# A second product of the down projection made of halved blocks, on one Trainium2 core

## The chip, the cores and the metric

The kernel runs on one core of a Trainium2 chip. The time is device microseconds (us) of one execution. Five engines run beside each other, each through its own list of instructions in order: TensorE (PE; its weight loads are listed apart as PEld), VectorE (DVE), ScalarE (ACT), GpSimd (POOL) and SyncE (SP), which here only issues transfers. Between them stand semaphores. Most transfers between DRAM and the on-chip memory are issued by SP, one behind the other.

## The reference

A decoder block in float32: sequence 1024, model width 1024. A pooling mixer and a sliding-window attention are merged by gates, then comes an MLP. The change touches only the MLP's two ends:

```python
    h2 = _rmsnorm(x, g_mlp_pre[l])
    ff = jnp.einsum('bsf,fd->bsd',
                    jnp.square(jax.nn.relu(jnp.einsum('bsd,df->bsf', h2, w_up[l]))), w_down[l])
    x = x + _rmsnorm(ff, g_mlp_post[l])
```

with w_up 1024 x 4096 and w_down 4096 x 1024. f below is the squared ReLU, 1024 x 4096.

## The kernel before

**Float32 out of faster passes.** Each operand of a matmul is split into a high and a low part of a reduced 32-bit format: `split` (L99) makes the high part by a CAST on ACT (L101) and the low part by a subtraction on DVE (L104). A product is then three passes: high by high, f's high by the weights' low, f's low by the weights' high (`PASSES`).

**Seven products instead of eight.** "Up" (the product with w_up) and "Down" (with w_down) are each made of 2 x 2 blocks, by a scheme that needs 7 products of half-size blocks and sums of blocks ahead of and behind them. Up's close, `up_close0` (L1614), forms the seven left operands out of f and stores them, 512 wide, into a scratch tensor in DRAM, `f_dram`; Down reads them back. The right operands are blocks B11, B12, B21, B22 of w_down or sums of them, made on DVE in the place where the blocks lie.

**Down.** Product i runs through 8 steps of the contraction, 56 steps in all, `PRODUCTS = (1, 5, 2, 3, 6, 7, 4)` (L2158). A usual step is 24 matmuls of 512 columns: 2 slices k2, 4 output tiles t, 3 passes (`down_mm`, L2071, matmuls recorded at L2075). The two parts of the left operand lie in tiles `wh`, those of the right in `ar`: six tiles of each, so three pairs. At step j, `ahead(j)` calls `operands` (L1963) for step j+2: SP loads the left block into a `raw` tile (four of them), ACT and DVE split both operands. A pair's tiles come free when the step that uses them ends.

**The sixth product** is not made so: its 512 x 512 blocks are halved once more and the same scheme is used within it, seven products of 256-wide blocks, `quarters` (L2021) for the operands, `quarters_mm` (L2043, matmuls at L2055) and `quarters_close` (L2059). A step is then 42 matmuls of 256 columns. Its operands are four sets of splits a step: f1 (128 x 1024, from `raw`), f2 (128 x 768, sums of quarters that Up has stored, from `raw`), w1 (128 x 512 and 128 x 256, from B11) and w2 (128 x 1024, from T, the sums of B11's quarters). They take two pairs of `wh` and two of `ar`, out of the same three.

**What sets the order.** A scheduler orders each engine's instructions from the program's order and its own costs, but where `manual_schedule` stands, DVE's follow the program's text: in Down before, for the operands of products 6, 7 and 4. `differences` (L2003), the sums of the blocks of w_down for products 3 to 4, is called all at once at the seventh step of product 3, and the scheduler spreads it over products 2 and 3. Product 3 adds onto product 5's banks of the accumulator memory, product 2 onto product 1's.

**Behind the products** come sums of their results, the norm's squares and gains (`fin_half`, `after_sixth`, `after_seventh`, `fin_out`), and for the last tile `last_tile` (L2124), whose DVE instructions end the execution.

## Time and profile before

| | us |
|---|---|
| median of 3 runs (1090.56 to 1091.35) | 1091.15 |
| the profiled execution's own time | 1091.0 |
| its span, first to last instruction | 1089.2 |
| PE busy | 1079.7 (99%) |
| DVE busy | 849.2 (78%) |
| ACT busy | 625.5 (57%) |
| Down, first matmul to PE's last | 779.1 to 1081.6 |
| the sixth product | 953.2 to 993.7 |

The page's first part sums each engine's busy time, the second shows it in 40 slices, the fourth follows the end back through what released it. A row of a timeline is: start, duration, engine, line, operation, output<-inputs, shape, how many in a row, and in square brackets the idle time ahead of it and what ended it. Pieces that follow each other on an engine overlap by some 0.1 us, as the pipeline does, so a cost in a row of work is read from start to start.

### The profile page before, as it was taken

The page shows a single profiled execution, that of the slowest core. Times are in us where ns is not written, and L with a number is a line of the kernel's source. Part 1 is how long each engine was busy: PE and PEld are TensorE (multiplying, and loading weights), DVE is VectorE, ACT ScalarE, POOL GpSimd, SP SyncE. Part 2 cuts the span into 40 slices and gives each one's busy share as a digit, 9 for nine tenths or more (in the row PEclk, how much of TensorE's full clock was granted, in tenths as well). Part 3 has the DMA queues.
Part 4 walks back from the last instruction along what each step waited for, and adds up shares of the span by engine and source line. Part 5 has one row for each costly group of instructions (what it writes and reads, how often), then busy time and mean ns, then how long its engine had stood idle before and what let it go on. Part 6 is the DMA issues. An engine that isn't in the chain of part 4 may idle for free.

```text
span 1089.2 us, 14332 instructions
## 1 busy us (share of the span) xinstructions
PE 1079.7 (99%) x5211; PEld 903.5 (83%) x5211; DVE 849.2 (78%) x1194; ACT 625.5 (57%) x1029; POOL 86.2 (8%) x142
## 2 busy tenths in 40 slices
PE   9999999999999999999999999999999999999997
PEld 8888888888888888888888888888888888898885
DVE  6688888989897887889876766665657867579996
ACT  7567886456654257567665554555446535476543
POOL 0354411100100012100000000000000000000000
PEclk9999999999999999999999999999999999999999
DMA  9666889679965776832566534445597873379622
GB/s 333 201 174 175 214 251 350 184 233 315 268 213 171 223 191 137 288 117 77 185 227 227 205 143 174 160 150 216 177 391 272 299 265 118 101 234 318 218 78 78
DMA packets 100921, 227.36 MB, mean 209 GB/s; under 512 B 10481, under 2 KB 28017, under 8 KB 100849
## 3 DMA queue, kind: packets, MB, share of 16 engines
q1 hardware_dynamic: 84416, 189.46, 50.8%
q0 software_dynamic: 10528, 16.78, 8.8%
q10 hardware_dynamic: 5904, 20.19, 4.8%
q8 instruction: 41, 0.67, 0.3%
q14 instruction: 32, 0.25, 0.1%
HBM read 161.38 MB, written 63.97 MB: 207 GB/s over the span
## 4 chain that ended last, share of the span: by engine, by line
PE 75%; DVE 4%; ACT 1%; issue 1%; DMA 1%; ACTq 0%; DVEq 0%
PE mm L583 18%; PE at L583 15%; PE at L2075 12%; PE mm L2075 11%; PE mm L1523 5%; PE mm L494 3%; PE at L2055 2%; PE at L1523 2%; PE at L1251 2%; PE mm L2055 2%; PE mm L1251 1%; PE mm L496 1%; PE at L1569 1%; DMA st<-in_w_g_dram 1%; DVE xf L2121 0%
## 5 line engine op out<-in xcount | busy, mean ns | idle before, releaser
L2075 PE MATMUL at<-ar,wh 128*128 128x512 f32 x552 | 126.0, 389 | 0.2 <-DVE ar L104 0.2
L2075 PEld LDWEIGHTS at<-ar,wh 128*128 128x128 f32 x552 | 103.4, 188 | 22.1 <-DVE ar L104 0.6
L2075 PE MATMUL mm<-ar,wh 128*128 128x512 f32 x528 | 120.5, 389 | 0.0
L2075 PEld LDWEIGHTS mm<-ar,wh 128*128 128x128 f32 x528 | 99.1, 188 | 20.5
L101 ACT CAST wh<-raw 128x1024 fp32r<-128x1024 f32 (+1 forms) x58 | 59.2, 1023 | 86.2 <-PE at L2075 37.0
L104 DVE TENSOR_TENSOR wh<-st,wh 128x512 fp32r<-128x512 f32 (+1 forms) x103 | 74.4, 733 | 38.9 <-ACT wh L101 34.3
L104 DVE TENSOR_TENSOR wh<-raw,wh 128x1024 fp32r<-128x1024 f32 (+1 forms) x58 | 68.4, 1186 | 40.8 <-ACT wh L101 40.6
L583 PE MATMUL mm<-T,wx 128*128 128x512 f32 x375 | 90.3, 389 | 0.0
L583 PEld LDWEIGHTS mm<-T,wx 128*128 128x128 f32 x375 | 70.4, 188 | 14.6
L583 PE MATMUL mm<-gr,wh 128*128 128x512 f32 x321 | 77.2, 391 | 0.0
L101 ACT CAST wh<-st 128x512 fp32r<-128x512 f32 (+2 forms) x102 | 65.8, 654 | 19.2 <-PE at L583 4.6
L583 PEld LDWEIGHTS mm<-gr,wh 128*128 128x128 f32 x321 | 59.9, 188 | 12.2
L583 PE MATMUL mm<-T,wh 128*128 128x512 f32 x267 | 66.0, 389 | 0.0
L104 DVE TENSOR_TENSOR ar<-B,ar 128x1024 fp32r<-128x1024 f32 (+2 forms) x51 | 50.9, 1011 | 14.7 <-ACT ar L101 14.4
L583 PE MATMUL at<-gr,wh 128*128 128x512 f32 x243 | 59.0, 389 | 0.0
L583 PE MATMUL mm<-x,wh 128*128 128x512 f32 x240 | 58.9, 394 | 0.0
L583 PEld LDWEIGHTS mm<-T,wh 128*128 128x128 f32 x267 | 50.1, 188 | 10.4
L101 ACT CAST ar<-B 128x1024 fp32r<-128x1024 f32 (+2 forms) x51 | 44.1, 882 | 19.3 <-PE mm L2055 6.4
L583 PEld LDWEIGHTS at<-gr,wh 128*128 128x128 f32 x243 | 45.6, 188 | 9.5
L583 PEld LDWEIGHTS mm<-x,wh 128*128 128x128 f32 x240 | 44.2, 188 | 9.6 <-ACT f L692 0.2
L583 PE MATMUL at<-T,wx 128*128 128x512 f32 x213 | 52.0, 389 | 0.0
L583 PEld LDWEIGHTS at<-T,wx 128*128 128x128 f32 x213 | 40.0, 188 | 8.3
(529 smaller groups left out, 2264.5 us busy)
## 6 DMA issues: line engine op xcount, KB each, us to landing
raw<-f_dram SPq DMA_DIRECT2D x52, 512.0 KB, 4.7
B<-in_w_dn_dram SPq DMA_DIRECT2D x32, 512.0 KB, 6.5
f_dram<-g SPq DMA_DIRECT2D x28, 512.0 KB, 2.8
st<-in_w_up_dram SPq DMA_DIRECT2D x24, 512.0 KB, 4.5
g<-spill_dram SPq DMA_DIRECT2D x17, 512.0 KB, 5.7
f_dram<-g ACTq DMA_DIRECT2D x17, 512.0 KB, 2.9
st<-in_w_g_dram SPq DMA_DIRECT2D x16, 512.0 KB, 4.7
g<-in_w_up_dram SPq DMA_DIRECT2D x15, 512.0 KB, 4.8
```

The source lines that it names most:

```text
L101: act.copy(hi, src)
L104: return eng.tensor_tensor(lo, src, f32(hi), ALU.subtract)
L494: pe.matmul(bs[th], whi[:, k, :], rhs(k, hl, th), start=k == 0 and hl == 0, stop=False)
L496: pe.matmul(bs[th], wlo[:, k, :], rhs(k, 0, th), start=False, stop=k == nk - 1)
L583: pe.matmul(b, w[wh][:, kt, :], x_, start=not after and kt == 0 and j == 0, stop=kt == 3 and j == 2, skip_group_check=after)
L1251: pe.matmul(b, w[wh][:, kt, :], xo[xh][:, kt, :], start=not after and kt == 0 and j == 0, stop=kt == 1 and j == 2, skip_group_check=after)
L1523: pe.matmul(bs[t], Am[a][k][ah][:, t * P:(t + 1) * P], Wm[w][k][wh], start=not after and k == 0 and j == 0, stop=k == 3 and j == 2, skip_g ...
L1569: pe.transpose(b[:, i, :], hs[4 * th + i][:, k * P:(k + 1) * P], ident)
L2055: pe.matmul(part[q][:, t, :], o[fs][fh][:, fk, t * P:(t + 1) * P], o[ws][wh][:, wk, :], start=q not in ONTO and (s_, t, j) == (0, 0, 0), s ...
L2075: pe.matmul(bs[t], fo[fh][:, k2, t * P:(t + 1) * P], wo_[wh][:, k2, :], start=not after and s2 == 0 and k2 == 0 and j == 0, stop=(s2, k2) ...
```

## The change

It does six things.

- The products' order is 1, 2, 5, 3, 6, 7, 4, and the fifth too is made as seven products of halved blocks (steps 16 to 23; the sixth stays at 32 to 39). `quarters`, `quarters_mm` and `quarters_close` take the product's number. The fifth's close writes four tiles `v4`.
- Up stores quarters' sums for the fifth as well as for the sixth (`e_dram(i, s)`), and splits the left operands of products 7 and 3 into high and low itself, in place; `f_dram` grows from 7 to 9 blocks. In Down the operands of these two products are loaded straight into `wh`, 2 x 512 KB a step (`WITH_PARTS`), where before one 512-KB load into `raw` was followed by a split.
- DVE's order in the whole of Down follows the text. The sums of blocks are called step by step: `first_sum` (B11 from B12 and B11) at steps 8 to 15, `quarter_sums` (T, three instructions) at 9 to 16 and 26 to 33, `next_sum` (B12, then B11) at 16 to 19 and 22 to 29, `last_sum` at 42 to 49.
- Loads of the weights' blocks are issued by a table of steps (`LOADS`), behind the load of that step's left operand.
- The tiles lie elsewhere: `raw` moves to the pool `rp`, B21, B22 and T share eight tiles "x".
- Product 3 has accumulator banks of its own and is added to v4 on DVE; the gains of `fin_half` and the squares of x1 move to steps 33 to 36 and 24 to 31; the operands of product 4's last three steps are made in another order.

```diff
             if m // 2 % 2 == 0:
-                dve.tensor_tensor(s2[:, 256:], s2[:, :256], s2[:, 256:], ALU.subtract)
-                s2_even.append(s2)
+                for b in (t[:, 0, :], s2):
+                    dve.tensor_tensor(b[:, 256:], b[:, :256], b[:, 256:], ALU.subtract)
+                evens.append(t)
             else:
-                a = s2_even.pop()
-                e = g32([3, 256])
-                dve.tensor_tensor(e[:, 1, :], s2[:, 256:], a[:, 256:], ALU.subtract)
-                dve.tensor_tensor(e[:, 0, :], e[:, 1, :], a[:, :256], ALU.add)
-                dve.tensor_tensor(e[:, 2, :], s2[:, :256], e[:, 1, :], ALU.subtract)
-                q.dma_start(e_dram(m // 4), e)
-            q.dma_start(fd[:, 4:6, :], t)
-            q.dma_start(fd[:, 0:2, :], f.rearrange("p (a b) -> p a b", b=512))
-            q.dma_start(fd[:, 6, :], s4)
+                t0 = evens.pop()
+                for i, a, b in ((5, t0[:, 0, :], t[:, 0, :]), (6, t0[:, 1, :], s2)):
+                    e = g32([3, 256])
+                    dve.tensor_tensor(e[:, 1, :], b[:, 256:], a[:, 256:], ALU.subtract)
+                    dve.tensor_tensor(e[:, 0, :], e[:, 1, :], a[:, :256], ALU.add)
+                    dve.tensor_tensor(e[:, 2, :], b[:, :256], e[:, 1, :], ALU.subtract)
+                    q.dma_start(e_dram(i, m // 4), e)
+            q.dma_start(fd[:, 5:7, :], t)
+            q.dma_start(fd[:, 0, :], f[:, :512])
+            for c, hi, lo in ((1, g[:, :512], f[:, 512:]), (7, s4[:, :512], s4[:, 512:])):
+                split(hi.bitcast(F32R), lo.bitcast(F32R), lo)
+                if c == 1:
+                    q.dma_start(fd[:, 1, :], hi)
+                    q.dma_start(fd[:, 2, :], lo)
+                else:
+                    q.dma_start(fd[:, 7:9, :], s4.rearrange("p (a b) -> p a b", b=512))
...
-    A_OF = {1: 0, 7: 1, 2: 2, 4: 3, 5: 4, 6: 5, 3: 6}
+    A_OF = {1: 0, 7: 1, 2: 3, 4: 4, 5: 5, 6: 6, 3: 7}
+    WITH_PARTS = (7, 3)
...
-    rpool = tc.tile_pool(name="rp", bufs=24, side="right", reuse_waits="tile")
+    rpool = tc.tile_pool(name="rp", bufs=16, side="right", reuse_waits="tile")
...
-        return dl.tile([P] + shape, F32, tag="raw", name=nm("raw"), bufs=4)
+        return rp.tile([P] + shape, F32, tag="raw", name=nm("raw"), bufs=4)
...
+    def held(name, dt=F32):
+        return dl.tile([P, 2, 512], dt, tag="x", name=nm(name), bufs=8)
...
+        if i in WITH_PARTS:
+            fo = wslot([2, 512]), wslot([2, 512])
+            for c, t in enumerate(fo):
+                behind[:] = [nc.sync.dma_start(f32(t), f_block(A_OF[i] + c, s_))]
+            ft = None
+        elif i == 1 and s_ in early_raw:
...
-    def differences(s_):
-        b11, b12, b22 = (res[n, s_] for n in ("B11", "B12", "B22"))
-        dve.tensor_tensor(b11, b22, b11, ALU.subtract)
-        w = halved(b11)
-        dve.tensor_tensor(b12, b22, b12, ALU.subtract)
-        tt = res["T", s_] = rp.tile([P, 4, 256], F32, tag="w", name=nm("T"))
+    def first_sum(s_):
+        dve.tensor_tensor(res["B11", s_], res["B12", s_], res["B11", s_], ALU.subtract)
+
+    def next_sum(n, s_):
+        dve.tensor_tensor(res[n, s_], res["B22", s_], res[n, s_], ALU.subtract)
+
+    def last_sum(s_):
+        dve.tensor_tensor(res["B11", s_], res["B21", s_], res["B11", s_], ALU.subtract)
+
+    def quarter_sums(s_):
+        w = halved(res["B11", s_])
+        tt = res["T", s_] = dl.tile([P, 4, 256], F32, tag="x", name=nm("T"), bufs=8)
         dve.tensor_tensor(tt[:, 0:2, :], w[:, 1::2, :], w[:, 0:2, :], ALU.subtract)
...
-        order = (5, 6, 1, 7, 3, 2, 4) if s_ == 0 else (5, 6, 3, 1, 7, 2, 4)
+    def quarters_mm(i, s_):
+        o = opers[i, s_]
+        onto = ONTO if i == 6 else {}
+        order = (5, 6, 3, 1, 7, 2, 4)
         if s_ == 0:
-            for q in (5, 6, 1, 7, 3, 2, 4):
-                part[q] = bank("mm" if q in ONTO else "at", [2, 256])
-                if q in ONTO:
+            order = (5, 6, 1, 7, 3, 2, 4) if i == 5 else (5, 6, 1, 3, 7, 2, 4)
+            mine, other = ("mm", "at") if i == 5 else ("at", "mm")
+            for q in order:
+                part[q] = bank(other if q in ONTO else mine, [2, 256])
+                if q in onto:
                     act.copy(part[q], block_of(u4, *ONTO[q]))
...
+        t4 = u4 if i == 6 else v4
+        w = block_of(t4, 2, 1)
         act.copy(a, part[1])
         dve.tensor_tensor(c, a, part[6], ALU.add)
         dve.tensor_tensor(e, c, part[5], ALU.add)
-        w = block_of(u4, 2, 1)
-        dve.tensor_tensor(w, w, part[5], ALU.add)
-        dve.tensor_tensor(d, c, part[7], ALU.add)
+        if i == 6:
+            dve.tensor_tensor(w, w, part[5], ALU.add)
+            dve.tensor_tensor(d, c, part[7], ALU.add)
+        else:
+            dve.tensor_tensor(d, c, part[7], ALU.add)
+            dve.tensor_tensor(w, d, part[5], ALU.add)
         for q, s in ((3, e), (2, a), (4, d)):
-            dve.tensor_tensor(block_of(u4, *ONTO[q]), s, part[q], ALU.add)
-        behind[:] = [dve.tensor_tensor(w, w, d, ALU.add)]
...
-    PRODUCTS = (1, 5, 2, 3, 6, 7, 4)
+    PRODUCTS = (1, 2, 5, 3, 6, 7, 4)
+    HALVED = (5, 6)
...
-        if (i, s_) == (3, NS - AHEAD):
-            for s2 in range(NS):
-                differences(s2)
...
+    TAGS = {1: ("at",) * 4, 3: ("at", "mm", "mm", "mm"), 7: ("mm", "at", "at", "at"), 4: ("at", "mm", "mm", "mm")}
+    banks = {}
+
+    LOADS = (("B11", 4, 3), ("B12", 5, 8), ("B22", 14, 8), ("B21", 41, 8))
+
+    def loads(j):
+        for name, first, n in LOADS:
+            if 0 <= j - first < n:
+                later(name, j - first)
+
+    def sums(j):
+        def at(first):
+            return 0 <= j - first < NS
+        if at(8):
+            first_sum(j - 8)
+        if at(9):
+            quarter_sums(j - 9)
+        if 16 <= j < 20 or 24 <= j < 28:
+            next_sum("B12", j - 16 - j // 24 * 4)
+        if at(22):
+            next_sum("B11", j - 22)
+        if at(26):
+            quarter_sums(j - 26)
+        if at(42):
+            last_sum(j - 42)
+
+    def ends(j):
+        if 33 <= j < 37:
+            fin_half(j - 33, 0, c11[j - 33])
+        if 24 <= j < 24 + NS:
+            square_x1(j - 24)
+        if j == 36:
+            scaled_eps()
+        if 40 <= j < 44:
+            after_sixth(j - 40)
+        if j in OUT_AT:
+            fin_out(OUT_AT.index(j), (c11, c12))
+        if 48 <= j < 52:
+            after_seventh(j - 48, banks[7][j - 48])
+
+    OUT_AT = (44, 45, 46, 47)
...
+    def ahead(j):
+        if j == 50:
+            operands(*steps[52])
+            operands(*steps[54])
+            operands(*steps[55])
+        elif j == 51:
+            operands(*steps[53])
+        elif j < 50:
+            operands(*steps[j + AHEAD])
...
+    with tc.manual_schedule(engines={mybir.EngineType.DVE}):
+        for j in range(1, AHEAD):
+            operands(*steps[j])
+        for j, step in enumerate(steps[:-1]):
+            down_step(j, *step)
+    down_step(len(steps) - 1, *steps[-1])
```

**The places in the order.** DVE in the sixth product before; B are blocks of w_down, T the quarters' sums, wh and ar the splits' outputs. Each step is f2, w2, w1 (two), f1:

```order
L104 TENSOR_TENSOR wh_8258<-raw_8243,wh_8257 128x1024
L104 TENSOR_TENSOR wh_8297<-raw_8294,wh_8296 128x768
L104 TENSOR_TENSOR ar_8299<-T_8201,ar_8298 128x1024
L104 TENSOR_TENSOR ar_8305<-B_1092_7125,ar_8304 128x512
L104 TENSOR_TENSOR ar_8305<-B_1092_7125,ar_8304 128x256
L104 TENSOR_TENSOR wh_8307<-raw_8292,wh_8306 128x1024
L104 TENSOR_TENSOR wh_8350<-raw_8347,wh_8349 128x768
L104 TENSOR_TENSOR ar_8352<-T_8207,ar_8351 128x1024
L104 TENSOR_TENSOR ar_8358<-B_1099_7163,ar_8357 128x512
L104 TENSOR_TENSOR ar_8358<-B_1099_7163,ar_8357 128x256
L104 TENSOR_TENSOR wh_8360<-raw_8345,wh_8359 128x1024
```

Splits alone stand here, step behind step. In the change, DVE in the fifth product, from f1 of step 17 on (L2020 to L2022 are `quarter_sums`, L2012 is `next_sum`):

```order
L104 TENSOR_TENSOR wh_7819<-raw_7804,wh_7818 128x1024
L2020 TENSOR_TENSOR T_7856<-B_1113_7374 128x512
L2021 TENSOR_TENSOR T_7856<-B_1113_7374,T_7856 128x256
L2022 TENSOR_TENSOR T_7856<-B_1113_7374,T_7856 128x256
L2012 TENSOR_TENSOR B_1119_7386<-B_1192_7773,B_1119_7386 128x1024
L104 TENSOR_TENSOR wh_7866<-raw_7863,wh_7865 128x768
L104 TENSOR_TENSOR ar_7868<-T_7620,ar_7867 128x1024
L104 TENSOR_TENSOR ar_7874<-B_1126_7424,ar_7873 128x512
L104 TENSOR_TENSOR ar_7874<-B_1126_7424,ar_7873 128x256
L104 TENSOR_TENSOR wh_7876<-raw_7861,wh_7875 128x1024
L2012 TENSOR_TENSOR B_1127_7426<-B_1204_7826,B_1127_7426 128x1024
L104 TENSOR_TENSOR wh_7940<-raw_7937,wh_7939 128x768
```

Between f1 of step 17 and f2 of step 18 stand four sums of blocks, and one L2012 more stands ahead of f2 of step 19; two further ones stand alike ahead of f2 of steps 20 and 21. In the change's sixth product, from f1 of step 33 to f2 and w2 of step 34:

```order
L104 TENSOR_TENSOR wh_8718<-raw_8703,wh_8717 128x1024
L2020 TENSOR_TENSOR T_8725<-B_1100_7300 128x512
L2021 TENSOR_TENSOR T_8725<-B_1100_7300,T_8725 128x256
L2022 TENSOR_TENSOR T_8725<-B_1100_7300,T_8725 128x256
L2020 TENSOR_TENSOR T_8732<-B_1106_7336 128x512
L2021 TENSOR_TENSOR T_8732<-B_1106_7336,T_8732 128x256
L2022 TENSOR_TENSOR T_8732<-B_1106_7336,T_8732 128x256
L104 TENSOR_TENSOR wh_8741<-raw_8738,wh_8740 128x768
```

Two steps' quarter sums stand here between the splits, where before none did; one more such group of three stands ahead of step 35's f2, one L2099 (a gain of `fin_half`) ahead of each of the f2 of steps 36 to 39, and four small instructions (`scaled_eps`) ahead of the last of these.

SP where the seventh product's first loads stand before (L1969; B are B21's blocks):

```order
L1969 DMA raw_8757<-f_dram 128x2x512
L1953 DMA B_1394_8932<-in_w_dn_dram 128x2x512
L1969 DMA raw_8868<-f_dram 128x2x512
L1969 DMA raw_8881<-f_dram 128x2x512
L1953 DMA B_1395_8934<-in_w_dn_dram 128x2x512
```

and SP where the third product's first loads stand in the change, behind the fifth's last ones:

```order
L2030 DMA raw_8203<-spill_dram 128x768
L1965 DMA B_1267_8157<-in_w_dn_dram 128x2x512
L1965 DMA B_1278_8223<-in_w_dn_dram 128x2x512
L1979 DMA wh_8268<-f_dram 128x2x512
L1979 DMA wh_8269<-f_dram 128x2x512
L1979 DMA wh_8373<-f_dram 128x2x512
L1979 DMA wh_8374<-f_dram 128x2x512
```

Two loads a step, L1979, go into `wh`, where before one into `raw` stood; so too for the seventh.

More of the change, by code (lines that the diff above doesn't have):

```diff
@@ L2102, in square_x1 @@
         t = flat(raw_tile())
-        nc.sync.dma_start(t, x1_dram[n])
+        with tc.issue_after(behind[0].ins):
+            nc.sync.dma_start(t, x1_dram[n])
         act.activation(t, t, AF.Square, scale=ROOT_D, accum_out=nsq[:, n:n + 1])
@@ new lines, in down_step @@
+    def down_step(j, i, s_):
+        last = s_ == NS - 1
+        normal = [(s_, k2, t) for k2 in range(2) for t in range(4)]
+        if i in HALVED and last:
+            with tc.manual_schedule(engines=CORE):
+                quarters_mm(i, s_)
+                quarters_close(i)
+            ahead(j)
+            sums(j)
+        elif i == 3 and last:
+            down_mm(i, s_, banks[i], False, normal)
+            for t in range(4):
+                dve.tensor_tensor(c12[t], v[t], banks[i][t], ALU.add)
+            ahead(j)
+            sums(j)
+        else:
+            sums(j)
+            ahead(j)
+        loads(j)
+        if i in HALVED:
+            if not last:
+                quarters_mm(i, s_)
+            ends(j)
+            return
+        if s_ == 0 and i in TAGS:
+            banks[i] = [bank(tag) for tag in TAGS[i]]
+        bs = banks[1 if i == 2 else i]
+        if (i, s_) != (3, NS - 1) and (i != 4 or s_ < NS - LATE):
+            down_mm(i, s_, bs, i == 2, normal[:3] + normal[4:7] if (i, s_) == (4, NS - LATE - 1) else normal)
+        ends(j)
+        if not last:
+            return
```

151 lines of the change are left out of this document (40 added, 111 removed).

## The prediction

> **What bounds the kernel now.** I read the page's first two parts, the stages' windows, the chain of waits over Down, then the engines' timelines there.
>
> ```profile
> PE 1079.7 (99%) x5211; PEld 903.5 (83%) x5211; DVE 849.2 (78%) x1194; ACT 625.5 (57%) x1029; POOL 86.2 (8%) x142
> PE   9999999999999999999999999999999999999997
> 953.00:994.00 41.00, 41.00 (x340) 40.81 (x339) 32.62 (x39) 32.14 (x45) 0.00 (x0) 1.00 0.78 255
> 994.00:1038.00 44.00, 43.79 (x193) 35.82 (x192) 42.72 (x56) 23.20 (x31) 0.00 (x0) 1.00 0.73 252
> ```
>
> PE works without a gap nearly to the end, so the time is the sum of its matmuls. Two things can count: cheaper or fewer matmuls, and gaps on PE that were not there. In the windows' rows (length, then busy PE, PEld, DVE, ACT, POOL, granted clock, DMA's share, GB/s) DVE is next behind PE in Down: busy 32.6 of 41 us in the sixth product, 42.7 of 44 after it. The chain of waits over Down shows each product's price:
>
> ```profile
> 779.30 43.52 PE at L2075 x192
> ...
> 909.86 43.52 PE mm L2075 x192
> 953.38 2.87 PE at L2055 x24
> ...
> 993.85 4.30 PE at L2075 x19
> 998.15 1.14 DVE wh L104
> 999.28 1.15 DVE ar L104
> 1000.47 37.47 PE at L2075 x164
> 1037.94 32.22 PE mm L2075 x142
> ```
>
> A usual product is 192 matmuls in 43.52 us, so 0.2267 us each and 5.44 us a step. The halved sixth lasts from 953.38 to 993.85, 40.47 us for 336 matmuls, so 0.120 us each and 5.04 us a step. The seventh, from 993.85 to 1037.94, takes 44.09 us: 0.57 more than 43.52, and two splits on DVE are in the chain there. They are the operands of its second step, behind the eight instructions of the sixth's close.
>
> **What a halved step leaves free on DVE.** This decides the forecast. DVE in the sixth, and ACT's row for the same kind of operand:
>
> ```profile
> 968.51 1.03 DVE L104 TENSOR_TENSOR ar<-B,ar 128x512 fp32r<-128x512 f32 x2
> 969.45 2.10 DVE L104 TENSOR_TENSOR wh<-raw,wh 128x1024 fp32r<-128x1024 f32 x2
> 971.47 1.22 DVE L104 TENSOR_TENSOR ar<-T,ar 128x1024 fp32r<-128x1024 f32 x1
> 973.54 1.03 DVE L104 TENSOR_TENSOR ar<-B,ar 128x512 fp32r<-128x512 f32 x2 [0.86 <-ACT ar L101]
> 962.81 0.93 ACT L101 CAST ar<-B 128x512 fp32r<-128x512 f32 x2 [1.26 <-PE mm L2055]
> ```
>
> From one w1 to the next, 968.51 to 973.54, are 5.03 us, a step. Of these 0.86 are idle, so the four sets of splits take 4.17. The idle time cannot be moved: w1 of the next step takes the tiles of this step's w1, ACT waits for PE to be done with them late in the step (1.26 in its row), and DVE for ACT. The operands begin at the step's end and must be done one step later. So a halved step has 0.86 us for other work on DVE; what exceeds it delays the next step's operands, and PE, which has nothing else to do, by as much. (A piece costs DVE some 0.09 less than its duration: the 1.03 at 968.51 is followed at 969.45.)
>
> **The change part by part.**
>
> 1. The fifth product halved: 43.52 becomes 336 x 0.120 = 40.3, so -3.2 us. The price of a halved matmul is seen in this trace:
>
> ```profile
> 953.22 3.04 PE L2055 MATMUL at<-ar,wh 128*128 128x256 f32 x24
> 956.09 2.32 PE L2055 MATMUL mm<-ar,wh 128*128 128x256 f32 x18
> ```
>
> 24 matmuls take 2.87 us from start to start, 0.120 each. The Trainium skill, "TensorE: Matmul & The Clock Gate", "Back-to-back issue gap", gives 262 cycles for 256 columns, an estimate of 0.109 us for each, but says too that in a stream the weight loads set the spacing as well. By 0.109 the fifth would take 36.7 and the saving be 6.9; the trace has 0.120 in the very stream that the change adds a second time, so the trace decides and the page's figure gets no chance of its own.
>
> 2. Sums of blocks between the halved splits. What they cost, from the groups of Down:
>
> ```profile
> L2007 DVE TENSOR_TENSOR B<-B,B 128x1024 f32<-128x1024 f32 x8 | 9.8, 1220 | 0.0
> L2009 DVE TENSOR_TENSOR T<-B 128x512 f32<-128x512 f32 x8 | 5.5, 690 | 0.2
> L2011 DVE TENSOR_TENSOR T<-B,T 128x256 f32<-128x256 f32 x8 | 3.4, 424 | 0.2
> L2010 DVE TENSOR_TENSOR T<-B,T 128x256 f32<-128x256 f32 x8 | 3.4, 422 | 0.2
> L2084 DVE TENSOR_TENSOR c<-c,bc 128x512 f32<-128x512 f32 x8 | 5.5, 690 | 1.6 <-ACT junk L2081 1.5
> 1079.83 0.16 DVE L144 TENSOR_TENSOR frr<-sm,sm 128x1 f32<-128x1 f32 x1
> ```
>
> Less 0.09 each: a block's sum 1.13, three quarter sums 0.60 + 0.33 + 0.33 = 1.27 (rounded), a gain 0.60; the small ones 0.16. In the changed order the fifth has T and a sum ahead of step 18's f2, 2.40, which is 1.54 over the 0.86, and one sum ahead of each of steps 19, 20 and 21, 0.27 over, 0.81 together: +2.35. The sixth has two T ahead of step 34's f2, 2.54, 1.68 over; one T ahead of step 35's, 0.41 over; a gain ahead of 36 to 38's, 0.60, which fits; a gain and four small ones ahead of 39's, 0.60 + 0.64, 0.38 over: +2.45. Together +4.8. A stall shifts every later step, DVE's splits too, so each counts in full. From below it is 0, if the splits can run further ahead than I read (rival A); from above 10.8, if none of the 0.86 can be used (2.40 + 3 x 1.13 + 2.54 + 1.27 + 1.24). The rows show the 0.86 idle in step after step and free for any work that needs no new operand, so I take 4.8. The sums also wait for their blocks of w_down, with all splits behind them on DVE; these are asked for two steps ahead, 10 us, and a block lands 5.5 us after its issue (quoted under 4): no wait. ACT's copies and squares of product 2's results, now between the first splits of the fifth, could make step 17 late by less than one copy, 0.59; taken as 0, since PE then waits a step earlier and DVE catches up by as much at step 18.
>
> 3. From the sixth to the seventh. Left operands come by DMA and only one split, 1.13, waits behind the close, where before two pairs stood in the chain; the 0.57 above should go: -0.6.
>
> 4. Loads straight into wh. At the third's and the seventh's first step the tiles come free only when step 22 or 38 ends, and 1 MB must land within one halved step, 5.04 us. The nearest rows are two loads issued 0.41 apart (start on SP's queue, and to landing):
>
> ```profile
> 869.47 0.37 SPq L1969 DMA_DIRECT2D raw<-f_dram  x1
> 869.88 0.46 SPq L1953 DMA_DIRECT2D B<-in_w_dn_dram  x1
> raw<-f_dram SPq DMA_DIRECT2D x1, 512.0 KB, 4.6
> B<-in_w_dn_dram SPq DMA_DIRECT2D x1, 512.0 KB, 5.5
> ```
>
> The high part, 4.6, is there in time. The low one lands 0.41 + 5.5 = 5.9 after the first issue; the step's third matmul wants it at 5.04 + 0.45. So 0.4 late each time with the traffic of those rows, nothing with an idle queue: from 0 to 0.9 each (0.9 if the weights' loads stand ahead), 0.15 taken, since the loads ahead of them in SP's list are a step older: +0.3. The Trainium skill, "DMA: Bandwidth & Descriptors", "Measured", has 6.15 us for 1 MB, another path; by it the loads would come 0.7 late each, +1.4. Later steps have two steps' time. Behind such a load SP has only x1's loads and the next step's, which have that time too.
>
> 5. The tail.
>
> ```profile
> 1077.39 0.68 DVE L2262 TENSOR_TENSOR u<-u,mm 128x512 f32<-128x512 f32 x1
> 1081.36 0.68 DVE L2139 TENSOR_TENSOR u<-u,mm 128x512 f32<-128x512 f32 x1
> 1080.68 0.88 PE L2136 MATMUL at<-hold,hold 128*128 128x256 f32 x6
> ```
>
> DVE's chain for the third of the last tiles takes 3.97 us, and last_tile's first sum follows it 0.2 ahead of PE's end. In the changed order the three tiles' chains stand wholly one behind the other, where before the first two were interleaved, and 15 instead of 18 matmuls of 512 columns lie behind the third tile's last: 0.68 us less cover. From 0 to 0.7, 0.45 taken.
>
> 6. Up's additions, in each of the 14 pairs (f's squares at L1663): two splits of 512, and one or three sums of 256. Prices, count and cover:
>
> ```profile
> L104 DVE TENSOR_TENSOR wx<-ws,wx 128x512 fp32r<-128x512 f32 x30 | 20.4, 687 | 0.0
> L101 ACT CAST wx<-ws 128x512 fp32r<-128x512 f32 x30 | 17.9, 618 | 7.7 <-DVE ws L535 6.1 <-PE at L583 1.6
> L1663 ACT ACTIVATE g<-g 128x1024 f32<-128x1024 f32 x14 | 14.9, 1061 | 0.1
> 600.00:700.00 100.00, 100.00 (x443) 82.84 (x442) 65.54 (x107) 53.74 (x86) 0.00 (x0) 1.00 0.48 174
> 700.00:779.00 79.00, 79.00 (x350) 65.42 (x349) 46.83 (x72) 40.82 (x61) 0.00 (x0) 1.00 0.49 178
> ```
>
> That is 2 x 0.60 + up to 3 x 0.33 = 2.2 us on DVE and 1.24 on ACT, some ten and six us more in 100, where DVE is idle for 34 and ACT for 46; the instructions stand behind the pair's close, whose results only Down reads, and what queues behind them, the next pair's splits, is made a pair ahead. Taken 0; rival C is the price without that cover. In the second and third products a step of 5.44 us holds three pieces of 1.13 and a T of 1.27, 4.66: it fits. The tiles' new places move no work on PE.
>
> Sum against the profiled execution's 1091.0, 0.15 under the median shown: 1091.0 - 3.2 + 4.8 - 0.6 + 0.3 + 0.45 = 1092.75, so **1092.7 us**.
>
> **The rivals.** A, the sums cost nothing: DVE's idle time lies wherever it is needed, since ACT may run further ahead than the rows show. 1092.75 - 4.8 = 1088.0. For it: DVE is busy for only 32.6 of 41 in the sixth, and 4.8 of other work would fill 37.4. Against it: the same idle 0.8 in every step, always ahead of w1 and for PE's sake; it cannot be saved up.
>
> B, slower: the loads into wh. They can only be issued when PE leaves the tiles, one step ahead. If both transitions get 5.9 or more, and the transfers are slowed by what is left of the blocks' loads, 0.9 each: 1092.75 - 0.3 + 1.8 = 1094.25. The point is a landing 5.5 us behind the issue of the first. For it: the row with 5.9. Against it: 512 KB alone lands within 4.6, and SP's queue has little ahead of them.
>
> C, Up: the added work makes a split late for PE in each of the 14 pairs by half of one, 0.3: 1092.75 + 4.2 = 1096.95. Against it: in Up's two rows PE is busy in every microsecond, with DVE idle for a third.
>
> **How the numbers follow.** The forecast has 0.50, A 0.22, B 0.21, C 0.07. The forecast alone spans 1091 to 1094: a third of the 4.8 either way, the tail's and the loads' ends within that. The range that leaves out no more than 2 in 10 goes from A, 1088.0, to past B, 1095.0; what lies outside are A's lower half, C, and the sums' upper bound. A measurement here cannot tell less than 0.2% from no change, 2.2 us: 1088.97 to 1093.33. Faster: A but for 0.02. Slower: B, C and 0.06 of the forecast's upper edge, 0.34. Same: the other 0.44 of the forecast and A's 0.02, 0.46.
>
> **What would show it.** Right: the fifth's matmuls at 0.120, 42 to a step; PE waits of 1 to 1.7 us at steps 18 and 34 with DVE L104 as what ended them, smaller ones at 19 to 21, 35 and 39; nothing missing between sixth and seventh. B: a wait for a DMA into wh at the third's or the seventh's first step. A: no waits in the fifth, the span 3 us shorter. Wrong would be a wait elsewhere: at a bank of the accumulators between two products, in Up, or of the seventh for B21.

## The result: 1% slower, and where the time went

The changed kernel takes 1100.9 us (median of 4 runs, 1100.59 to 1102.7) beside 1090.96 for the kernel before (1090.56 to 1091.35): a ratio of 1.0095, with a 95% interval of 1.0077 to 1.0112. I had forecast 1092.7, in a range up to 1095.0. The profiled execution took 1100.61, its span is 1098.8.

The page's first part, after:

```profile
PE 1080.4 (98%) x5355; PEld 907.8 (83%) x5355; DVE 890.6 (81%) x1301; ACT 636.6 (58%) x1062; POOL 84.9 (8%) x142
```

PE's busy time did not fall by the 3.2 us that the fifth product should save, and the span without PE, 9.5 us before, is 18.4. Part of the waits hides in the busy time: PE's row at 876.16, for instance, has 12 halved matmuls in 1.86 us, where the next such row takes 1.60. PE's timeline names the longer waits; these are its rows from Up to the end that have idle time of 0.3 us or more in brackets:

```profile
562.60 2.56 PE L583 MATMUL mm<-T,wx 128*128 128x512 f32 x10 [0.32 <-DVE wx L104]
591.21 0.74 PE L583 MATMUL mm<-T,wx 128*128 128x512 f32 x2 [1.34 <-ACT wx L101]
881.34 1.46 PE L2064 MATMUL mm<-ar,wh 128*128 128x256 f32 x10 [1.05 <-DVE ar L104]
902.09 1.57 PE L2064 MATMUL mm<-ar,wh 128*128 128x256 f32 x11 [0.53 <-DVE ar L104]
913.29 0.71 PE L2090 MATMUL at<-ar,wh 128*128 128x512 f32 x2 [1.00 <-DMA wh<-f_dram]
970.07 1.45 PE L2064 MATMUL at<-ar,wh 128*128 128x256 f32 x10 [1.30 <-DVE ar L104]
975.66 1.45 PE L2064 MATMUL at<-ar,wh 128*128 128x256 f32 x10 [0.31 <-DVE ar L104]
1002.81 0.50 PE L2090 MATMUL mm<-ar,wh 128*128 128x512 f32 x1 [1.02 <-DMA wh<-f_dram]
1073.53 1.43 PE L2090 MATMUL at<-ar,wh 128*128 128x512 f32 x5 [0.61 <-DVE ar L104]
```

L2064 are the halved matmuls, L2090 the usual ones. From the first matmul of each product in the two timelines, a budget of the two spans (us):

| stretch | before | after | difference |
|---|---|---|---|
| start to Down's first matmul | 779.1 | 781.9 | +2.8 |
| two usual products, first in Down | 87.0 | 87.1 | 0 |
| the fifth, up to the third's first matmul (43.5 as a usual product) | 43.5 | 44.3 | +0.8 |
| the third | 43.5 | 44.0 | +0.5 |
| the sixth | 40.5 | 43.3 | +2.9 |
| seventh and fourth, to PE's end | 87.9 | 89.6 | +1.7 |
| PE's end to DVE's last row | 3.3 | 4.1 | +0.8 |

The halved fifth alone lasts from 868.97 to 912.14 (the start of its last row, 910.70, and 12 matmuls of 0.120), 43.2 us and not 40.3. So almost nothing of the saving is left, and every other stretch that the change touches got longer.

**The halved steps.** The length of each step less 5.04 us, from the counts of 42 matmuls in PE's rows, against the forecast (16 and 23 in the fifth and 32, 37 and 38 in the sixth lost nothing):

| step | 17 | 18 | 19 | 20 | 21 | 22 | 33 | 34 | 35 | 36 | 39 |
|---|---|---|---|---|---|---|---|---|---|---|---|
| forecast | 0 | 1.54 | 0.27 | 0.27 | 0.27 | 0 | 0 | 1.68 | 0.41 | 0 | 0.38 |
| measured | 0.25 | 1.30 | 0.17 | 0.17 | 0.18 | 0.79 | 0.38 | 1.56 | 0.55 | 0.20 | 0.34 |

4.8 us were forecast, 5.9 measured. DVE while PE is in steps 18 and 19 of the fifth, the changed kernel:

```profile
883.27 1.22 DVE L2012 TENSOR_TENSOR B<-B,B 128x1024 f32<-128x1024 f32 x1
884.41 0.95 DVE L104 TENSOR_TENSOR wh<-raw,wh 128x768 fp32r<-128x768 f32 x1
885.28 1.22 DVE L104 TENSOR_TENSOR ar<-T,ar 128x1024 fp32r<-128x1024 f32 x1
886.41 1.02 DVE L104 TENSOR_TENSOR ar<-B,ar 128x512 fp32r<-128x512 f32 x2
887.35 1.22 DVE L104 TENSOR_TENSOR wh<-raw,wh 128x1024 fp32r<-128x1024 f32 x1
888.49 1.22 DVE L2012 TENSOR_TENSOR B<-B,B 128x1024 f32<-128x1024 f32 x1
```

No row has a bracket: DVE has no idle time, and its list repeats every 5.22 us, from one L2012 to the next. That is the length of PE's steps 19 to 21, so DVE sets PE's pace there. At step 22, where nothing was forecast, 0.79 us were lost, and DVE waits:

```profile
899.94 0.96 DVE L104 TENSOR_TENSOR wh<-raw,wh 128x768 fp32r<-128x768 f32 x1 [0.94 <-ACT wh L101]
```

**The loads.** SP's rows at the passage from the fifth to the third, the changed kernel:

```profile
907.17 0.37 SPq L1979 DMA_DIRECT2D wh<-f_dram  x1
907.63 0.42 SPq L1979 DMA_DIRECT2D wh<-f_dram  x1
909.37 0.36 SPq L1979 DMA_DIRECT2D wh<-f_dram  x1
```

The two parts for step 24 are asked for at 907.17 and 907.63, when step 22 ends. The chain of waits has the second parts of the two passages, this one and the one to the seventh:

```profile
907.63 6.89 DMA wh<-f_dram
995.75 7.01 DMA wh<-f_dram
```

The first of them lands at 914.5, and PE's third row of step 24 starts then (914.56). So a second part takes 6.9 to 7.0 us from its own issue, where the prediction had 5.5, and lands 7.4 behind the first part's issue, where it had 5.9. What made it slower is not settled. The loads for step 25 follow already at 909.37, as PE reaches the middle of step 23 and leaves their tiles, and a load of a weights' block (issued at 906.18) is still under way. But the pair from which the prediction took its 5.5, issued at 869.47 and 869.88 in the kernel before, had two loads as close behind it:

```profile
871.74 0.37 SPq L1958 DMA_DIRECT2D raw<-in_w_dn_dram  x1
872.15 0.46 SPq L1953 DMA_DIRECT2D B<-in_w_dn_dram  x1
```

The transfer engines were busy for 0.92 of the time there (869.4 to 875.5), for 0.82 at the passage to the third (907.1 to 914.6) and 0.97 at that to the seventh (995.3 to 1002.9).

**Up.** The weights' next load (L523) stands behind stores in SP's list. The same place before, and after:

```profile
551.40 0.48 SPq L523 DMA_DIRECT2D g<-in_w_up_dram  x1
```

```profile
554.00 0.32 SPq L1645 DMA_DIRECT2D spill_dram<-g  x1
554.38 0.42 SPq L523 DMA_DIRECT2D g<-in_w_up_dram  x1
558.73 0.69 DVE L532 TENSOR_TENSOR ws<-g 128x512 f32<-128x512 f32 x1 [3.44 <-DMA g<-in_w_up_dram]
```

DVE waits 3.44 us for that load, with all splits behind it, and PE gets the wait of 0.32. The one of 1.34 us at 591.21 comes later; DVE's waits ahead of it are for PE's result and for a later load (issued at 582.96):

```profile
586.74 0.69 DVE L625 TENSOR_TENSOR f<-f,at 128x512 f32<-128x512 f32 x1 [3.49 <-PE at L583]
588.35 0.69 DVE L532 TENSOR_TENSOR ws<-g 128x512 f32<-128x512 f32 x1 [0.93 <-DMA g<-in_w_up_dram]
```

### The profile page after: what moved, and what is told of

Same layout as the page of the kernel before. It is cut to its first block, busy times and chain, and to the rows that moved or that the text cites. A ratio compares the mean times of both kernels' runs of the same rounds, so it can differ in the third digit from the quotient of the medians.

```text
span 1098.8 us, 14946 instructions
## 1 busy us (share of the span) xinstructions
PE 1080.4 (98%) x5355; PEld 907.8 (83%) x5355; DVE 890.6 (81%) x1301; ACT 636.6 (58%) x1062; POOL 84.9 (8%) x142
## 4 chain that ended last, share of the span: by engine, by line
PE 82%; DVE 7%; DMA 5%; ACT 3%; issue 2%; SPq 0%; DVEq 0%; ACTq 0%
PE mm L583 25%; PE at L583 18%; PE at L2090 10%; PE mm L1523 5%; PE mm L494 3%; PE mm L2090 2%; PE sc L182 2%; PE at L1523 2%; PE at L1251 2%; PE mm L191 2%; PE mm L182 2%; PE mm L2064 2%; PE at L2064 2%; DVE wh L104 2%; PE mm L1251 1%
## 5 line engine op out<-in xcount | busy, mean ns | idle before, releaser
L2090 PE MATMUL at<-ar,wh 128*128 128x512 f32 x588 | 141.2, 390 | 1.7 <-DMA wh<-f_dram 1.0
L2090 PEld LDWEIGHTS at<-ar,wh 128*128 128x128 f32 x588 | 110.2, 188 | 25.5 <-ACT ar L101 1.2
L104 DVE TENSOR_TENSOR wh<-st,wh 128x512 fp32r<-128x512 f32 (+1 forms) x103 | 74.3, 730 | 40.9 <-ACT wh L101 37.1
L101 ACT CAST wh<-raw 128x1024 fp32r<-128x1024 f32 (+1 forms) x50 | 48.8, 980 | 56.8 <-PE at L2090 41.5
L2090 PE MATMUL mm<-ar,wh 128*128 128x512 f32 x300 | 76.0, 390 | 1.0 <-DMA wh<-f_dram 1.0
L104 DVE TENSOR_TENSOR wh<-raw,wh 128x1024 fp32r<-128x1024 f32 (+1 forms) x50 | 56.6, 1135 | 24.3 <-ACT wh L101 24.2
L2090 PEld LDWEIGHTS mm<-ar,wh 128*128 128x128 f32 x300 | 56.2, 188 | 13.0 <-DMA wh<-f_dram 1.5
L2064 PE MATMUL at<-ar,wh 128*128 128x256 f32 x336 | 48.5, 284 | 1.8 <-DVE ar L104 1.6
```

What stands on the lines that cost most here:

```text
L101: act.copy(hi, src)
L104: return eng.tensor_tensor(lo, src, f32(hi), ALU.subtract)
L2064: pe.matmul(part[q][:, t, :], o[fs][fh][:, fk, t * P:(t + 1) * P], o[ws][wh][:, wk, :], start=q not in onto and (s_, t, j) == (0, 0, 0), s ...
L2090: pe.matmul(bs[t], fo[fh][:, k2, t * P:(t + 1) * P], wo_[wh][:, k2, :], start=not after and s2 == 0 and k2 == 0 and j == 0, stop=(s2, k2) ...
```

## The experiments

Twelve kernels were run. "Down's start" is its first matmul in the profiled execution.

**The sums on GpSimd.** Four B12 sums and four T are called with `pool` in place of `dve`:

```diff
-            next_sum("B12", j - 16 - j // 24 * 4)
+            next_sum("B12", j - 16 - j // 24 * 4, dve if j >= 24 else pool)
...
-            quarter_sums(j - 26)
+            quarter_sums(j - 26, dve if j < 31 else pool)
```

> The changed kernel, but the sums of blocks that stand between the halved products' splits on DVE (four of B12 at steps 16 to 19, T of the fifth's last step, T of the sixth's last three steps) are made on GpSimd, which has nothing else to do in Down; all that is computed stays. Theory S: PE's waits in the halved products come from DVE's list, a step's 4.17 us of splits plus these sums being more than 5.04 us. Then the fifth, 43.17 us in the changed kernel, and the sixth, 43.33, come to 40.3 to 41.2 each, and the time from 1100.9 to 1095.0 to 1096.5. Rival: the splits wait for their loads or for ACT, and the sums only fill DVE's waiting time. Then both stay within 0.5 us of what they were, and the time stays at 1100 to 1101.

1100.36 (1099.46 to 1102.33): no gain, and in a way that neither theory had. The sixth came down from 43.3 to 41.8, most of the way to theory S's 41.2, but the fifth with the passage to the third went up from 44.3 to 46.6. GpSimd's and DVE's rows there:

```profile
892.14 2.95 POOL L2012 TENSOR_TENSOR B<-B,B 128x1024 f32<-128x1024 f32 x1 [2.21 <-DMA B<-in_w_dn_dram]
```

```profile
892.75 3.43 DVE L104 TENSOR_TENSOR ar<-T,ar 128x1024 fp32r<-128x1024 f32 x1
896.10 1.01 DVE L104 TENSOR_TENSOR ar<-B,ar 128x512 fp32r<-128x512 f32 x2
```

A split that takes 1.22 alone takes 3.43 beside GpSimd's sum, 2.2 more, about the 2.34 during which both run. So DVE stood still for most of that time: a sum taken off its list, where it cost 1.13, cost it 2.2. The Trainium skill, "SBUF — State Buffer", "Terms", says that DVE and GpSimd share a pair of ports, that one of them holds it for a full instruction, and that the other is blocked meanwhile; the trace agrees, with 2.2 us of delay in 2.34 of overlap. In the sixth the sums on GpSimd ran during the third (939 to 955), where DVE had room. The run does not decide on the fifth.

**The sums left out.** The four B12 sums are not made, and an older T is used in the fifth's last step and the sixth's last three:

```diff
-        if 16 <= j < 20 or 24 <= j < 28:
-            next_sum("B12", j - 16 - j // 24 * 4)
+        if 24 <= j < 28:
+            next_sum("B12", j - 20)
...
+        if older:
+            res["T", s_] = last_t[0]
+            return
```

> The changed kernel without the sums between the halved products' splits: the four B12 sums at steps 16 to 19 are left out (the first four steps of product 7 then use B12 itself), and the last T of the fifth and the last three of the sixth are left out, an older T standing in for them; nothing takes their place on any engine. Theory S (DVE's list is too long for a halved step): the fifth goes from 43.2 to 40.4 to 40.9 us, the sixth from 43.3 to 40.4 to 41.0, the time from 1100.9 to 1095.2 to 1096.2. Rival: the splits wait for loads or for ACT; then each stays above 42.5 and the time above 1099.5.

1096.09 (1095.08 to 1097.44), 4.8 less. The fifth takes 40.7 (868.51 to 909.21, counted as the 43.2 was), the sixth 40.9. Theory S holds: of the 5.9 us lost in the halved steps the sums bring 4.8 to 4.9.

**The room priced in the kernel before.** First with two needless sums ahead of each f2 of the sixth:

```diff
+        for _ in range(2):
+            dve.tensor_tensor(extra, gfin_b[:, :512], gfin_b[:, 512:], ALU.add)
         split(*f2, fs)
```

> The kernel before, with two needless sums of 128 x 512 on DVE, 0.60 us each, ahead of the f2 split of each step of the sixth product; nothing else is changed. This prices the room that a halved step has on DVE. By the 0.86 us of idle time in the trace of before, 1.20 is 0.34 over in the 7 or 8 steps: the time goes from 1090.9 to 1093.2 to 1093.7. By the steps of the changed kernel that had one sum of 1.13 and lasted 5.21 us instead of 5.04, the room is 0.96 and the excess 0.24: 1092.5 to 1092.9. Rival: DVE has more room than its idle time says: 1090.5 to 1091.3.

1090.52 (1090.2 to 1091.51), no change; but it tests nothing. Its trace has all 16 sums between 787 and 805, at Down's start: they read nothing that is made late, and the scheduler had put them there. So a second time, each reading the f1 split just made:

```diff
+        for _ in range(2 if s_ else 0):
+            dve.tensor_tensor(extra, f32(opers[6, s_ - 1][0][1])[:, 0:2, :], gfin_b[:, :512].rearrange(...), ALU.add)
         split(*f2, fs)
```

> The kernel before, with two needless sums of 128 x 512 on DVE (0.60 us each) between f1 and the next f2 of the sixth product, seven times; each reads the f1 split ahead of it, so that it cannot be made earlier. (In the run with the two sums that read only the gains, the scheduler had put them at the start of Down, where they hid.) By the 0.86 us of idle time, 1.20 is 0.34 over, seven times: 1090.9 becomes 1093.0 to 1093.6. By the changed kernel's steps with one sum, where DVE without a pause took 5.21 us, so 4.08 for the splits: 0.24 over, 1092.3 to 1092.9. Rival: DVE has room for it all the same, 1090.5 to 1091.3.

1093.35 (1092.85 to 1093.66), ratio 1.0021, interval 1.0012 to 1.003. DVE's rows in the sixth:

```profile
965.47 1.42 DVE L2029 TENSOR_TENSOR extra<-wh,bc 128x512 f32<-128x512 f32 x2
966.81 0.95 DVE L104 TENSOR_TENSOR wh<-raw,wh 128x768 fp32r<-128x768 f32 x1
967.68 1.22 DVE L104 TENSOR_TENSOR ar<-T,ar 128x1024 fp32r<-128x1024 f32 x1
968.81 1.02 DVE L104 TENSOR_TENSOR ar<-B,ar 128x512 fp32r<-128x512 f32 x2
969.75 1.22 DVE L104 TENSOR_TENSOR wh<-raw,wh 128x1024 fp32r<-128x1024 f32 x1
971.00 1.42 DVE L2029 TENSOR_TENSOR extra<-wh,bc 128x512 f32<-128x512 f32 x2
```

The time agrees with the expectation by 0.86, but the rows say it differently: a step of DVE lasts 5.53, and the two sums, which wait for the split ahead and for each other, take 1.46 and not 1.20 (969.75 to 971.00 is 1.25 for a split of 1.13, and 965.47 to 966.81 is 1.34). So the splits take 4.07 and the room is 0.97; 1.46 less 0.97 is the 0.49 by which a step is longer. That is also what the changed kernel's steps 19 to 21 say: 5.22 less 1.14 for the sum (883.27 to 884.41) is 4.08.

> As the run with two needless sums, but with one, 0.60 us, seven times. It fits into the 0.86: 1090.6 to 1091.3, no change. Rival: whatever is added in a halved step delays PE by as much, 7 x 0.6: 1095.

With one sum 1090.73 (1089.81 to 1091.0), ratio 0.9996 (0.9987 to 1.0005): it fits, as expected.

**The first loads into other tiles.**

```diff
-            fo = wslot([2, 512]), wslot([2, 512])
+            fo = [wslot([2, 512]) if s_ else rp.tile([P, 2, 512], F32R, tag="raw", ...) for c in (0, 1)]
```

> The changed kernel, but the left operand of the first step of the third and of the seventh product is loaded into raw tiles, which come free some 3 us before PE leaves the wh tiles; all that is computed stays. Theory D: PE stands still ahead of these two products (1.15 and 0.5 us at the third, 1.0 and 0.4 at the seventh) because the loads can be issued only when PE leaves the tiles, and take 6 to 7 us. Then both waits go, and the time falls by 2.5 to 3.2, to 1097.7 to 1098.4. Rival: PE waits for the right operand, whose split stands behind the last quarters' splits on ACT and DVE; then it falls by less than 0.8.

1097.94 (1096.83 to 1098.62), 3.0 less. PE's timeline at the two passages:

```profile
912.58 1.60 PE L2064 MATMUL at<-ar,wh 128*128 128x256 f32 x12
914.02 0.86 PE L2090 MATMUL at<-ar,raw 128*128 128x512 f32 x3
...
999.66 1.60 PE L2064 MATMUL mm<-ar,wh 128*128 128x256 f32 x12
1001.10 0.86 PE L2090 MATMUL mm<-ar,raw 128*128 128x512 f32 x3
```

No idle time at either; theory D holds. From the first matmuls, the two passages and the third are 3.0 us shorter: 1.2 up to the third, 0.5 in it, and 1.4 in the seventh, which now takes 43.55. That the whole time fell by the same 3.0 is partly luck: in this trace the fourth is 0.7 shorter too, with the wait at 1073.5 gone, and Up is 2.3 longer. I had expected neither. All later operands take the wh tiles a turn earlier here; that this is why the wait went isn't shown.

**Up.** Four runs vary what it makes and what it stores. The stores on GpSimd's queue:

```diff
-            q = nc.sync if m < NF - 2 else nc.scalar
+            q = nc.gpsimd if m < NF - 2 else nc.scalar
```

> The changed kernel, but Up's stores of the left operands are issued by GpSimd and not by SP; all that is computed stays. Theory Q: Up became 2.2 us longer (Down's first matmul at 781.9 instead of 779.1, 0.5 of it from the first 150 us) because SP issues a pair's stores, which now wait for more work of DVE and ACT, ahead of the next weights' loads, so that these come late (a load at 554.4 that stood at 551.4 before). Then Down begins at 779.4 to 780.0 and the time falls by 1.9 to 2.5, to 1098.4 to 1099.0. Rival: DVE's and ACT's added work itself makes the splits late. Then Down begins at 781.5 to 782.2 still, and the time stays within 0.5.

1102.57 (1099.38 to 1103.9), Down's start at 783.49: no gain. SP's list then holds only the weights' loads in this stretch, and its waits there are for tiles, 55.5 us for DVE's splits to leave them and 10.3 for stores to land. Theory Q, SP's order alone, gets no support.

The splits gone from Up altogether (Down loads the two operands whole and splits them):

```diff
-    WITH_PARTS = (7, 3)
+    WITH_PARTS = ()
...
-            for c, hi, lo in ((1, g[:, :512], f[:, 512:]), (7, s4[:, :512], s4[:, 512:])):
-                split(hi.bitcast(F32R), lo.bitcast(F32R), lo)
...
+            q.dma_start(fd[:, 0:2, :], f.rearrange("p (a b) -> p a b", b=512))
+            q.dma_start(fd[:, 7, :], s4[:, 512:])
```

> The changed kernel with the fifth halved as it is, but without the splits in Up: the left operands of products 3 and 7 are stored whole, loaded into raw, and split in Down as in the kernel before; all that is computed stays. Up keeps the quarters' sums for the fifth. If the splits and their stores are what made Up longer, Down begins at 779.4 to 780.0; if the quarters' sums are, at 781 or later. The waits for a transfer into wh go, 2.5 to 3.2. Against that, DVE has 5.8 us of work in a 5.44-us step of the third at four steps, 1.4 more, and the close of the sixth stands ahead of two pairs of splits again, 0.6. Sum: 1100.9 - 2.2 - 2.9 + 2.0 = 1097.8, if no other wait comes.

1094.96 (1094.83 to 1095.12), Down's start at 779.39. So the quarters' sums for the fifth cost Up little, and the waits for transfers are gone; the third lasts 45.2 us instead of 43.5, more than the 1.4 expected of DVE's list.

The splits made, but only the high part stored of each, which Down splits again (it leaves the low parts out):

> The changed kernel, in which Up still splits the left operands of products 3 and 7, but stores only the high part, one block each, so that Up stores as many blocks as without the splits; Down loads that block, and splits it as the kernel before does. It leaves out the low parts of these two operands. Theory W (the splits' own work on DVE and ACT, 2.2 and 1.2 us in a pair, makes Up's weights late): Down's first matmul stays at 781.5 to 784. Theory M (the two more blocks stored per pair, 0.5 MB, fill SP's list and the DMA engines): it goes to 779.3 to 780.2. Without the splits and their stores it was 779.4.

1095.91 (1095.69 to 1095.92), Down's start at 779.85. And the stores, doubled, without the splits (`q.dma_start(fd[:, c, :], lo)` and the same into `c + 1`):

> The changed kernel without the splits in Up, but with as many stores and bytes as it has: the left operands of products 3 and 7 are stored whole, twice each; Down loads one copy and splits it. Theory M (the stores themselves: with the splits, and the stores of one part, Down began at 779.85; with neither at 779.4): Down's first matmul at 781.5 to 784, the time 2 to 4 us above the 1095.0 of the kernel with neither. Rival: it needs the splits and the stores together, so that a store waits for a split and holds up SP's list; then Down begins at 779.4 to 780.3 and the time is 1095 to 1095.8.

1096.71 (1096.45 to 1096.97), Down's start at 780.37; the first two products of Down take 88.1 us here instead of 87.0, for a reason that was not followed up. The stretch from 560 to 620 us, where Up loses most, in the windows (length, PE, PEld, DVE, ACT, POOL, clock, DMA's share, GB/s): before, then the change, then without splits, splits alone, stores alone, each from its own trace:

```profile
560.00:620.00 60.00, 60.00 (x266) 49.71 (x265) 47.07 (x81) 35.27 (x57) 0.00 (x0) 1.00 0.55 200
```

```profile
560.00:620.00 60.00, 58.34 (x255) 47.14 (x254) 51.26 (x92) 40.24 (x65) 0.00 (x0) 1.00 0.74 263
```

```profile
560.00:620.00 60.00, 60.00 (x265) 49.16 (x264) 49.95 (x89) 36.15 (x59) 0.00 (x0) 1.00 0.58 211
```

```profile
560.00:620.00 60.00, 59.52 (x260) 48.21 (x259) 54.40 (x97) 40.52 (x67) 0.00 (x0) 1.00 0.62 224
```

```profile
560.00:620.00 60.00, 59.33 (x261) 48.44 (x261) 49.05 (x87) 36.46 (x59) 0.00 (x0) 1.00 0.73 259
```

Down's start alone misleads by up to 0.6 us, since the traces differ already before PE has lost anything in Up: the matmul that starts at 545.22 in the kernel before starts between 544.61 and 545.40 in the others. Counted from that matmul to Down's first one, the stretch takes 233.92 us before and, in single traces, longer by:

| Up of the run | us longer |
|---|---|
| without the splits (the quarters' sums alone) | 0.45 |
| the splits, one part stored | 1.32 |
| the stores, without the splits | 1.43 |
| both: the changed kernel | 2.74 |
| both: with the sums left out of Down | 2.79 |
| both: with the sums on GpSimd | 3.55 |
| both: with the first loads in raw tiles | 5.00 |

So beyond the quarters' sums the splits alone cost 0.9 us, the stores alone 1.0, and both together 2.3 to 4.6 with the same Up. Neither theory W nor M holds alone. Both together cost more than their sum, in the changed kernel by 0.4 only; by what path stays open. A store that waits for a split holds SP's list and holds its tile, and the weights' loads need both; the run on GpSimd's queue, where the stretch is 4.5 longer, speaks for the tiles, but its stores take another way as well. No run gives the loads a tile more.

**The causes taken away together**, with all of the computation kept: the sums placed where no halved step pays for them, the third's first operand in raw tiles, only the third's operands split in Up.

```diff
-        if 16 <= j < 20 or 24 <= j < 28:
-            next_sum("B12", j - 16 - j // 24 * 4)
...
+        for n in {24: (0, 1), 25: (2, 3), 26: (4,), 27: (5,), 28: (6,), 29: (7,)}.get(j, ()):
+            next_sum("B12", n)
+        for n in {30: (6, 7)}.get(j, (j - 24,) if 24 <= j < 30 else ()):
+            quarter_sums(n)
...
-    WITH_PARTS = (7, 3)
+    WITH_PARTS = (3,)
```

> The changed kernel with three causes taken away at once, all of the computation kept: no sum stands between the halved products' splits (B12's first four sums at steps 24 and 25, each T one or two steps earlier, the small ones of the gains' step two steps later), the first left operand of the third product is loaded into raw tiles, and only the third's left operands are split in Up, the seventh's in Down as before. If the three theories hold: 1100.9 less 5.0 for the sums, 3.0 for the loads, 1.4 to 2.8 for half to all of Up's loss, plus 0.6 for the seventh's start: 1090.7 to 1092.1. If the time falls by less than 6, a wait elsewhere takes over, above all DVE in the third, whose list is then full: 43.5 us of work in 43.5.

1091.92 (1091.45 to 1093.08), ratio to the kernel before 1.0011, interval 1.0002 to 1.002: 9.0 us of the 9.9 are back. The fifth takes 40.9, the sixth 40.7, so the halving does save what it should; the third takes 44.7, 1.2 too long, with DVE busy for 44.1 of it; Up is still 2.0 longer by the count from 545, and the tail is 0.6 longer than before. With the last step of product 4 in the text's order as well (`manual_schedule(engines=CORE)` around it):

> The kernel with the three causes taken away, and in addition the last step of product 4 in the text's order on PE, DVE and ACT, so that 18 matmuls of 512 columns stand behind the third tile's last one instead of 15. If the tail is a matter of this cover, DVE's last chain starts some 0.3 us ahead of PE's end instead of 0.6 behind it, and the time falls from 1091.9 to 1090.9 to 1091.4; if not, it stays at 1091.6 to 1092.2.

1092.0 (1091.52 to 1093.59), no change. DVE's chain for the last tile starts 0.30 us ahead of PE's end (1083.06 and 1083.36) where it stood 0.37 behind it in the run ahead: the tail behaves as reckoned. But a wait of 0.82 us on PE, for a split of product 4, has come at 1065.5, and the fourth is 0.9 us longer. No version beat the kernel before.

## Why the prediction was wrong, step by step

- **Halving the fifth, -3.2: right within 0.6.** With the causes taken away it takes 40.9 us, 2.6 less than a usual product; the matmuls cost the 0.120 each that the trace of before had.
- **The room of 0.86 us and the sums, +4.8: right in kind and nearly in size.** Leaving the sums out gave 4.8 back. The room is 0.97, measured in two kernels: step 19's 1.13 less 0.97 is 0.16, and 0.17 were measured. Why the idle time in a row, 0.86, is not quite the room isn't shown; DVE presumably does without some of it when its operands wait for it rather than it for them. The halved steps lost 1.1 more, most of it at step 22 (0.79), where DVE waited 0.94 us for ACT. ACT's cast began at 899.07, when the load issued at 893.85 had landed (5.1 us; the same load a step earlier took 3.4). That load is asked for only when a split has left its raw tile, and the splits run late. In the kernel without the sums the load for this step is nearly as slow, 4.9 us, and DVE waits 0.87 for ACT there, but PE does not wait: there the splits have that much to spare. The prediction followed the delay from DVE to PE and not back through the loads; why this load is slower than its neighbours stays open.
- **Loads straight into wh, +0.3: the first step that failed.** It cost 3.0 by the run with raw tiles (forecast, both passages: 0.3; rival B: 1.8). The term that was mis-sized is the landing: the second part was to land 5.9 us behind the first part's issue and landed 7.4 behind it, at both passages. I had the place right, had a price for nothing worse than 0.9 each, and took a value near its lower end with no row behind it. The next step's pair, issued 2.2 us later, I had named and left out of the price; but the row that I went by had two loads as close behind it (so its 4.6 is not that of a load alone either); the next pair by itself does not explain the difference, and its cause stays open. A wider look was at hand in the sixth part of the page of before, which gives the median landing of each kind of load:

```profile
raw<-f_dram SPq DMA_DIRECT2D x52, 512.0 KB, 4.7
B<-in_w_dn_dram SPq DMA_DIRECT2D x32, 512.0 KB, 6.5
```

With 6.5 in place of 5.5 each passage is 1.4 late, 2.8 together. No run has a load "with an idle queue", for which I had put nothing.
- **From the sixth to the seventh, -0.6: right, but not to be seen.** With the first loads in raw tiles the seventh takes 43.55 us instead of 44.09. In the changed kernel the wait for the transfer (1.02 us in PE's row) stands in that place, and it takes 44.9.
- **Up, 0: the second step that failed.** It cost 2.7 to 5.0. The step said that the added work has idle time enough and that what queues behind it is made a pair ahead. I had set that work against DVE's and ACT's idle share over the whole stretch, and had no price for the stores. The runs show loads of the weights that are asked for later (554.38 instead of 551.40) and DVE waiting for them. Neither splits nor stores alone cost more than 1.0 us; together they cost 2.3 and more. Rival C's price, 4.2, was near, but not its mechanism, half a split in each of 14 pairs: nearly all is lost between 545 and 620, and PE has no bracket from there to Down.
- **The tail, +0.45:** 0.78. DVE's last chain starts 0.6 behind PE's end and not 0.2 ahead of it, and the run with the last step in the text's order put it ahead again: the mechanism given.
- **Not foreseen:** 0.61 us of wait at step 53, in product 4, for a split.
- **The range.** I had set the sums, the loads and Up beside each other as alternatives, each with a chance of its own, and none with another. But none of them excludes another, and all three places lost time. Forecast, rival B's and rival C's added prices make 1092.75 + 1.5 + 4.2 = 1098.5; the range had to reach there at least, and ended at 1095.0.

## What to carry to other kernels

When the bounding engine has no idle time, a cheaper product is worth what the feeding engines can still feed in its shorter step: take the room from the step's length less the feeder's work back to back, and count each added instruction against it, step by step. A transfer that may start only when its tile comes free has no slack: price it by all the landings on record and not by the nearest row (5.5 us here, with a median of 6.5 on the page and 6.9 and 7.0 measured). Added stores and added work ahead of them may cost little each and more together (0.9, 1.0 and 2.3 us here). Delays that do not exclude each other add up: give the range their sum, not the largest of them.

## What the runs showed of the hardware

- A sum of 128 x 1024 on GpSimd takes 2.4 to 2.95 us, and a DVE split of 1.22 us beside it takes 3.43: moving such work off a full DVE made the fifth longer, 46.6 us instead of 44.3.
- Two dependent DVE instructions follow each other some 0.13 us later than independent ones (1.25 instead of 1.13 behind a split, 1.34 instead of 1.20 for two sums into one tile).
- With the same Up and small differences in Down's text, Down began at 781.4 to 783.8, and Up was 2.7 to 5.0 us longer than before, so a single trace of that stage is good to some two microseconds.
